# Strassen's products on twelve instead of eight of 32 channel blocks in both layers' ways out

## The chip, the cores and the metric

The kernel runs on one core of one Trainium2 chip. The metric is the device time of one execution in microseconds (us). The kernel before takes 1362.15 us, the median of 3 runs (1361.92 to 1362.23).

## What is computed

Two decoder layers on 256 tokens of width 2048, in float32:

```python
def retention_layer(x, g_norm, w_in, gn, w_out):
    ...                      # norm, q/k/v/gate projection, 8 heads of retention
    return o @ w_out         # (256 x 4096) @ (4096 x 2048)

def pooling_layer(x, g_norm, w_in, w_grp, b_grp, scale, w_out):
    ...                      # norm, branch/gate projection, causal pooling, 4 groups
    return (mix * jax.nn.silu(z)) @ w_out    # (256 x 4096) @ (4096 x 2048)

def reference(x, ...):
    h = x + retention_layer(x, ...)
    h = h + pooling_layer(h, ...)
    return rms_norm(h, final_norm)
```

The change concerns the two products with `w_out`, the "ways out" of the layers.

## The kernel before, in words

Every float32 value that a matmul reads is split in a rounded high part (a CAST on ScalarE, L98) and the rest (a subtract on VectorE, L99), and a product of two such pairs takes three matmuls: high by high, high by low, low by high (`Sum.add`, L195). Weights come in units of 128 x 2048 values, one DMA of 1 MB each, and a plain unit is split in two halves of 1024 columns. The pairs live in five rotating buffers (`w`), the raw units in three.

A way out (`way_out`) has two passes, one for each half of the 2048 output columns, and each pass sixteen units in the order of the string `ORDER`:

- A **C unit** holds four blocks of 128 channels by 512 columns. It goes to one column quarter: four blocks, two halves of the tokens (t), three matmuls each, so 24 matmuls of 512 columns.
- An **S unit** holds two blocks of channels by two column quarters, as the four corners of a two by two product with the two token halves (t). Strassen's way in Winograd's form takes seven products instead of eight: 21 matmuls in place of 24. VectorE pays for it: sums of weights (`s`, L221, 1024 columns; L223 and L224, 512 columns each), and four pairs (1024, 512, 1024 and 1024 columns) in place of two (1024 each).
- The sums of the activations that S units need (`forms`) are made once for each layer, in the first pass, by `sides` (L198 to L215), one call for two S units: an add of 1024 columns (L202), then four adds or subtracts of 256 columns (L208 to L214) and four splits of 256 columns (L99 again).

The eight sums of a pass (`p1`, `p5`, `p6`, `p7`, `c11`, `c21`, `c12`, `c22`) take all eight PSUM banks. After the last S unit VectorE adds the p's and two of the c's into the residual stream `xn` (`add`, L481, and L517, L520), while TensorE works on the C units that are left; these go to `c12` and `c22`, whose adds come last. In layer 1 each piece of 512 columns that is complete is squared and then turned by TensorE for the next layer (`turn`, L554 and L562). In layer 2 the last two C units are held and multiplied token half by token half, and each piece goes through the final norm (`norm`, L664 to L692, with a multiply on GpSimd, L671).

Before layer 1's way out stands the last head of the retention, whose output `og` TensorE turns (L453) for the blocks 28 to 31 of `os`. The buffer `tmp`, which `sides` writes first (L202), lies in memory that was `gz` and its neighbours in the heads, so that `sides` starts after those last turns. Instructions of one engine run in the order in which a scheduler has put them when the program was built; a read or write that depends on another engine waits on a semaphore.

Of the kernel before, what the change touches and what calls it, by code (L numbers as in the profile page):

```python
# [13 lines left out]
P = 128  # L14
# [11 lines left out]
UNIT = 2048  # L26
HALF = UNIT // 2

ORDER = "CCCCSCSCCSCSCCCC"
NS = ORDER.count("S")  # L30
CLASSIC = ((0, 0), (0, 1), (1, 0), (2, 0), (3, 0), (1, 1), (4, 0), (5, 0), (2, 1), (3, 1), (4, 1), (5, 1))
FIRST = (20, 16)
SUMS = ("p1", "p5", "p6", "p7", "c11", "c21", "c12", "c22")


# [15 lines left out]
def kernel(  # L51
# [44 lines left out]
    def split(hi, lo, src):  # L96

        nc.scalar.copy(hi, src)  # L98
        nc.vector.tensor_tensor(out=lo, in0=src, in1=hi.bitcast(F32), op=ALU.subtract)  # L99
# [87 lines left out]
    class Sum:  # L187
# [5 lines left out]
        def add(self, a_hi, a_lo, w_hi, w_lo):  # L193
            for a, w in ((a_hi, w_hi), (a_hi, w_lo), (a_lo, w_hi)):
                nc.tensor.matmul(self.tile, a, w, start=(self.done == 0), stop=(self.done == self.n - 1))  # L195
                self.done += 1

    def sides(A, first, i, a, s, forms):  # L198


        blocks = A[:, first + 4 * i : first + 4 * i + 4]
        nc.vector.tensor_tensor(out=a, in0=blocks[:, :, 0].bitcast(F32), in1=blocks[:, :, 1].bitcast(F32), op=ALU.add)  # L202
        a11, a21, a12, a22 = a[:, :2, :P], a[:, :2, P:], a[:, 2:, :P], a[:, 2:, P:]

        def put(form, src):
            split(forms[:, 2 * i : 2 * i + 2, form, 0], forms[:, 2 * i : 2 * i + 2, form, 1], src)

        nc.vector.tensor_tensor(out=s, in0=a21, in1=a22, op=ALU.subtract)  # L208
        put(0, s)
        nc.vector.tensor_tensor(out=a21, in0=a11, in1=a21, op=ALU.subtract)  # L210
        put(2, a21)
        nc.vector.tensor_tensor(out=s, in0=s, in1=a11, op=ALU.subtract)
        put(1, s)
        nc.vector.tensor_tensor(out=s, in0=s, in1=a12, op=ALU.add)  # L214
        put(3, s)  # L215
# [37 lines left out]
    with tc.tile_pool(name="rt", bufs=1) as rt:  # L253
# [62 lines left out]
        unit = 4  # L316


        forms = os[:, VT - 4 :].rearrange("p k a s -> p (k a s)").rearrange("p (i f l t) -> p i f l t", f=4, l=2, t=P)

        def tokens(k, t):
            ts = slice(t * P, (t + 1) * P)
# [137 lines left out]
    def way_out(A, src, first, forms, tmp, work, y, after, ends=False):  # L460
# [4 lines left out]
        def blk(k, t):  # L465
            ts = slice(t * P, (t + 1) * P)
            return A[:, k, 0, ts], A[:, k, 1, ts]

        for p in range(2):
# [20 lines left out]
            for n, kind in enumerate(ORDER):  # L490
                unit = src[p * len(ORDER) + n]
                if kind == "C":
                    u = (next(classic), weights(unit))
                    if ends and p == 1 and n >= len(ORDER) - 2:
                        held.append(u)
                    else:
                        rows(u, 0)
                        rows(u, 1)
                    if p == 0 and n in (1, 3):
                        a = tmp[:, : 4 * S].rearrange("p (k s) -> p k s", s=S)  # L500
                        sides(A, first, n // 2, a, tmp[:, 4 * S : 4 * S + 2 * P].rearrange("p (k s) -> p k s", s=P), forms)
                    if not ends and n == 5:
                        for c in (2 * p, 2 * p + 1):
                            tc.keep_in_program_order(nc.gpsimd.dma_start(out=y(None, c), in_=xN[:, :, c * 512 : (c + 1) * 512]))
                    continue
                raw = load(unit)
                s = [work.tile([P, 2, 512], F32, tag=f"s{i}", name=f"s{i}") for i in range(2)]
                k1, k2 = strassen_blocks(first, strassen)
                strassen_unit(raw, s, (blk(k1, 0), blk(k2, 0), blk(k2, 1)), forms[:, strassen], sums)
                strassen += 1  # L510
                if strassen == NS:
                    u = tmp[:, 4 * S + 2 * P :]
                    nc.scalar.copy(u, sums["p1"].tile)
                    add(0, 0, ALU.add, sums["c11"].tile)
                    add(0, 0, ALU.add, u)
                    after(0, 2 * p)
                    nc.vector.tensor_tensor(out=u, in0=u, in1=sums["p6"].tile, op=ALU.add)  # L517
                    add(0, 1, ALU.subtract, u)
                    add(1, 0, ALU.add, sums["c21"].tile)
                    nc.vector.tensor_tensor(out=u, in0=u, in1=sums["p7"].tile, op=ALU.add)  # L520
                    add(1, 0, ALU.add, u)
                    after(1, 2 * p)
                    add(0, 1, ALU.add, sums["p5"].tile)
                    add(1, 1, ALU.add, sums["p5"].tile)
                    add(1, 1, ALU.subtract, u)
# [10 lines left out]
    with tc.tile_pool(name="pl", bufs=1) as pl:  # L536
# [8 lines left out]

        with tc.tile_pool(name="work1", bufs=1) as work:
            tmp = pl.tile([P, 4 * S + 2 * P + 512], F32, tag="gz", name="tmp")
            forms = pl.tile([P, NS, 4, 2, P], F32R, tag="ms", name="forms")
            hs2 = act.tile([P, KT, 2, S], F32R, tag="hs", name="hs2")

            def turn(t, c):
                y = stream(t, c)
# [139 lines left out]
                nc.sync.dma_start(out=out[t][:, ps], in_=piece)  # L692

        with tc.tile_pool(name="work2", bufs=1) as work:
            tmp = act.tile([P, 4 * S + 2 * P + 512], F32, tag="hs", name="tmp")
            forms = pl.tile([P, NS, 4, 2, P], F32R, tag="ms", name="forms")
            way_out(gs, pool_out, FIRST[1], forms, tmp, work, stream, norm, True)


# [119 lines left out]
```

## Time and profile before

| what | value |
|---|---|
| median of 3 runs | 1362.15 us |
| the profiled execution's own time | 1361.73 us |
| its span, first to last instruction | 1359.4 us |
| PE busy | 1347.6 us, 99% |
| DVE (VectorE) busy | 1073.6 us, 79% |
| ACT (ScalarE) busy | 731.6 us, 54% |
| POOL (GpSimd) busy | 25.5 us, 2% |

The profile's engines are PE (TensorE), DVE (VectorE), ACT (ScalarE), POOL (GpSimd) and SP (the queue that issues loads). Successive instructions overlap a little, so a group's busy time is longer than its share of the engine; where an engine runs without a pause, the time from one start to the next start is what an instruction costs. The clock that was granted to TensorE is given for each stretch as a share of its full 2.4 GHz.

### The profile page before, as it was taken

The page shows a single profiled execution, that of the slowest core. Times are in us where ns is not written, and L with a number is a line of the kernel's source. Part 1 is how long each engine was busy: PE and PEld are TensorE (multiplying, and loading weights), DVE is VectorE, ACT ScalarE, POOL GpSimd, SP SyncE. Part 2 cuts the span into 40 slices and gives each one's busy share as a digit, 9 for nine tenths or more (in the row PEclk, how much of TensorE's full clock was granted, in tenths as well). Part 3 has the DMA queues.
Part 4 walks back from the last instruction along what each step waited for, and adds up shares of the span by engine and source line. Part 5 has one row for each costly group of instructions (what it writes and reads, how often), then busy time and mean ns, then how long its engine had stood idle before and what let it go on. Part 6 is the DMA issues. An engine that isn't in the chain of part 4 may idle for free.

```text
span 1359.4 us, 17755 instructions
## 1 busy us (share of the span) xinstructions
PE 1347.6 (99%) x6846; PEld 1145.6 (84%) x6846; DVE 1073.6 (79%) x1550; ACT 731.6 (54%) x1031; POOL 25.5 (2%) x34
## 2 busy tenths in 40 slices
PE   9999999999999999999999999999999999999997
PEld 7888888888888888878888888888888888888886
DVE  7868787878787878798677867876886896888676
ACT  7455555555555555555555545445545545555444
POOL 0000000000000000000000000000000000000102
PEclk9999999999999999999999999999999999999999
DMA  8555546464645455575556555555555555555552
GB/s 338 182 192 174 203 164 213 161 217 161 213 164 200 171 193 177 188 247 201 181 185 213 188 190 187 190 200 190 196 190 186 187 188 192 191 207 212 186 214 95
DMA packets 38196, 262.64 MB, mean 193 GB/s; under 512 B 4368, under 2 KB 4496, under 8 KB 7392
## 3 DMA queue, kind: packets, MB, share of 16 engines
q1 hardware_dynamic: 36432, 255.41, 54.3%
q0 software_dynamic: 1536, 5.57, 1.3%
q8 instruction: 54, 0.88, 0.2%
q10 hardware_dynamic: 144, 0.52, 0.1%
q14 instruction: 30, 0.25, 0.0%
HBM read 259.39 MB, written 2.10 MB: 192 GB/s over the span
## 4 chain that ended last, share of the span: by engine, by line
PE 98%; DVE 1%; ACT 0%; DMA 0%; issue 0%; DVEq 0%; SPq 0%; ACTq 0%
PE c L195 43%; PE acc L129 29%; PE acc L130 15%; PE p L195 6%; PE po L427 1%; PE acc L286 1%; PE acc L287 1%; PE turned L453 1%; PE sc L352 0%; DMA xin<-in_ret_in 0%; PE sc L357 0%; ACT w L98 0%; PE turned L562 0%; DVE w L99 0%; DVE tsin L339 0%; DVE tcos L338 0%
## 5 line engine op out<-in xcount | busy, mean ns | idle before, releaser
L99 DVE TENSOR_TENSOR w<-raw,w 128x1024 fp32r<-128x1024 f32 x472 | 558.1, 1192 | 140.7 <-ACT w L98 136.4
L98 ACT CAST w<-raw 128x1024 fp32r<-128x1024 f32 x472 | 479.1, 1026 | 275.5 <-PE c L195 172.8
L129 PE MATMUL acc<-hs,w 128*128 128x512 f32 x1472 | 516.3, 394 | 0.0
L130 PE MATMUL acc<-hs,w 128*128 128x256 f32 x1472 | 413.4, 281 | 0.0
L129 PEld LDWEIGHTS acc<-hs,w 128*128 128x128 f32 x1472 | 275.7, 187 | 61.8
L195 PE MATMUL c<-w,hs 128*128 128x512 f32 x1284 | 303.9, 390 | 0.0
L195 PEld LDWEIGHTS c<-w,hs 128*128 128x128 f32 x1284 | 239.1, 188 | 49.6
L130 PEld LDWEIGHTS acc<-hs,w 128*128 128x128 f32 x1472 | 278.0, 189 | 1.8
L195 PE MATMUL c<-w,os 128*128 128x512 f32 x666 | 162.6, 392 | 0.0
L195 PE MATMUL c<-w,gs 128*128 128x512 f32 x624 | 147.1, 390 | 0.0
L195 PEld LDWEIGHTS c<-w,os 128*128 128x128 f32 x666 | 124.4, 188 | 26.8 <-ACT w L98 0.3
L195 PEld LDWEIGHTS c<-w,gs 128*128 128x128 f32 x624 | 117.0, 188 | 24.8
L138 ACT COPY hl<-acc 128x256 f32<-128x256 f32 x96 | 35.6, 372 | 147.2 <-PE acc L130 147.2
L129 PE MATMUL acc<-ms,w 128*128 128x512 f32 x256 | 89.0, 390 | 0.0
L130 PE MATMUL acc<-ms,w 128*128 128x256 f32 x256 | 72.2, 282 | 0.0
L98 ACT CAST w<-s 128x1024 fp32r<-128x1024 f32 x32 | 33.5, 1049 | 53.9 <-PE c L195 48.6
L99 DVE TENSOR_TENSOR w<-s,w 128x1024 fp32r<-128x1024 f32 x32 | 39.1, 1223 | 24.6 <-ACT w L98 24.5
L129 PEld LDWEIGHTS acc<-ms,w 128*128 128x128 f32 x256 | 48.0, 188 | 10.1
L130 PEld LDWEIGHTS acc<-ms,w 128*128 128x128 f32 x256 | 48.4, 189 | 0.0
L195 PE MATMUL p<-w,os 128*128 128x512 f32 x150 | 40.9, 390 | 0.0
L195 PE MATMUL p<-w,forms 128*128 128x512 f32 x144 | 39.8, 397 | 0.5 <-ACT forms L98 0.5
L195 PEld LDWEIGHTS p<-w,forms 128*128 128x128 f32 x144 | 27.0, 188 | 7.5 <-ACT forms L98 1.0
(184 smaller groups left out, 1024.7 us busy)
## 6 DMA issues: line engine op xcount, KB each, us to landing
raw<-in_ret_in SPq DMA_DIRECT2D x92, 1024.0 KB, 5.0
raw<-in_pool_in SPq DMA_DIRECT2D x64, 1024.0 KB, 5.0
raw<-in_ret_out SPq DMA_DIRECT2D x32, 1024.0 KB, 5.0
raw<-in_pool_out SPq DMA_DIRECT2D x32, 1024.0 KB, 5.1
raw<-in_pool_grp SPq DMA_DIRECT2D x16, 1024.0 KB, 5.0
xin<-in_ret_in SPq DMA_DIRECT2D x3, 1024.0 KB, 11.4
xn<-in_xN POOLq DMA_DIRECT2D x4, 512.0 KB, 6.8
out<-xn SPq DMA_DIRECT2D x8, 256.0 KB, 2.3
```

The source lines that it names most:

```text
L98: nc.scalar.copy(hi, src)
L99: nc.vector.tensor_tensor(out=lo, in0=src, in1=hi.bitcast(F32), op=ALU.subtract)
L129: nc.tensor.matmul(acc, hi, moving[:, k], start=(k == 0), stop=False)
L130: nc.tensor.matmul(acc[:, :S], lo, moving[:, k, 0], start=False, stop=(k == n - 1))
L138: nc.scalar.copy(t, acc[:, S:])
L195: nc.tensor.matmul(self.tile, a, w, start=(self.done == 0), stop=(self.done == self.n - 1))
L286: nc.tensor.matmul(accs[c], hi[:, b], hs[:, k], start=(k == 0), stop=False)
L287: nc.tensor.matmul(accs[c][:, :S], lo[:, b], hs[:, k, 0], start=False, stop=(k == KT - 1))
L427: nc.tensor.matmul(po[t], ss[:, p, queries], vs[:, keys, q], start=first, stop=last)
L453: nc.tensor.transpose(turned[:, j * S + t * P : j * S + (t + 1) * P], og[:, t, (2 * i + j) * P : (2 * i + j + 1) * P], idt)
```

## The change

The order of a pass goes from twelve C units and four S units to ten and six, with the two in turn in the middle. The first and the last units of a pass stay plain, three and two of them in place of four and four. The S units' channel blocks now begin at 16 (layer 1) and 12 (layer 2). A third call of `sides` makes the forms of the added pair; in layer 1 these lie in the part of `hs2` that layer 2's input fills later, in layer 2 forms and `tmp` have changed places. The calls of `sides` come after the units 0, 2 and 4 of the first pass, in place of 1 and 3, and the load of `x` after unit 4 in place of 5.

```diff
-ORDER = "CCCCSCSCCSCSCCCC"
+ORDER = "CCCSCSCSCSCSCSCC"
 NS = ORDER.count("S")
-CLASSIC = ((0, 0), (0, 1), (1, 0), (2, 0), (3, 0), (1, 1), (4, 0), (5, 0), (2, 1), (3, 1), (4, 1), (5, 1))
-FIRST = (20, 16)
+CLASSIC = ((0, 0), (0, 1), (1, 0), (2, 0), (3, 0), (1, 1), (2, 1), (4, 0), (3, 1), (4, 1))
+FIRST = (16, 12)
...
+    def forms_at(blocks):
+        return blocks.rearrange("p k a s -> p (k a s)").rearrange("p (i f l t) -> p i f l t", f=4, l=2, t=P)
...
-            split(forms[:, 2 * i : 2 * i + 2, form, 0], forms[:, 2 * i : 2 * i + 2, form, 1], src)
+            split(forms[:, :, form, 0], forms[:, :, form, 1], src)
...
-                    if p == 0 and n in (1, 3):
+                    if p == 0 and n in (0, 2, 4):
                         a = tmp[:, : 4 * S].rearrange("p (k s) -> p k s", s=S)
-                        sides(A, first, n // 2, a, ..., forms)
-                    if not ends and n == 5:
+                        sides(A, first, n // 2, a, ..., forms[n // 2])
+                    if not ends and n == 4:
...
-            forms = pl.tile([P, NS, 4, 2, P], F32R, tag="ms", name="forms")
+            forms = pl.tile([P, 4, 4, 2, P], F32R, tag="ms", name="forms")
             hs2 = act.tile([P, KT, 2, S], F32R, tag="hs", name="hs2")
+            forms = [forms[:, :2], forms[:, 2:], forms_at(hs2[:, 8:12])]
...
-            tmp = act.tile([P, 4 * S + 2 * P + 512], F32, tag="hs", name="tmp")
-            forms = pl.tile([P, NS, 4, 2, P], F32R, tag="ms", name="forms")
+            tmp = pl.tile([P, 4 * S + 2 * P + 512], F32, tag="ms", name="tmp")
+            forms = act.tile([P, 6, 4, 2, P], F32R, tag="hs", name="forms")
+            forms = [forms[:, 2 * i : 2 * i + 2] for i in range(3)]
```

The added lines shift the numbers behind L198 by four or five: L202 is L206 in the changed kernel, L453 is L457, L481 is L485, L562 is L567.

**First place.** TensorE, layer 1's first pass, around the last turns of the retention (L453, in the changed kernel L457). `turned` is what TensorE writes when it turns `og`; `p1`, `p5` and `p7` are sums of the first S unit, `c11` and `c21` sums that C units share. Before:

```order
L453 MATMUL turned_4648<-idt_297,og_4641 128x128 x3
L453 MATMUL turned_4657<-idt_297,og_4641 128x128 x3
L195 MATMUL c21_4683<-w_4768,os_352 128x512 x3
L195 MATMUL c11_4682<-w_4797,os_352 128x512 x6
L195 MATMUL c11_4682<-w_4800,os_352 128x512 x6
L195 MATMUL c21_4683<-w_4797,os_352 128x512 x6
L195 MATMUL c21_4683<-w_4800,os_352 128x512 x6
L195 MATMUL p1_4678<-w_4845,os_352 128x512 x3
L195 MATMUL c11_4682<-w_4850,os_352 128x512 x3
L195 MATMUL p5_4679<-w_4853,forms_4676 128x512 x2
```

The change:

```order
L195 MATMUL c21_4683<-w_4768,os_352 128x512 x5
L457 MATMUL turned_4648<-idt_297,og_4641 128x128
L457 MATMUL turned_4657<-idt_297,og_4641 128x128
L195 MATMUL c21_4683<-w_4768,os_352 128x512
L457 MATMUL turned_4648<-idt_297,og_4641 128x128 x3
L457 MATMUL turned_4657<-idt_297,og_4641 128x128 x3
L195 MATMUL p1_4678<-w_4813,os_352 128x512 x3
L195 MATMUL c11_4682<-w_4818,os_352 128x512 x3
L195 MATMUL p5_4679<-w_4821,forms_4676 128x512 x2
L195 MATMUL p7_4681<-w_4821,forms_4676 128x512 x2
```

Between the last turn and the first matmul that reads `forms` stood 33 matmuls; now 6 stand there, and three of the others come ahead of the turns.

**Second place.** TensorE, the end of layer 1's second pass and the start of layer 2's first projection (`acc`, L129 and L130); `turned` (L562, now L567) is a piece of `xn`. Before, from the last C unit on:

```order
L195 MATMUL c22_5322<-w_5872,os_352 128x512 x6
L195 MATMUL c22_5322<-w_5875,os_352 128x512 x6
L129 MATMUL acc_5953<-hs2_4677,w_5947 128x512
L130 MATMUL acc_5953<-hs2_4677,w_5947 128x256
...
L562 MATMUL turned_5908<-idt_297,xn_4670 128x128
L562 MATMUL turned_5917<-idt_297,xn_4670 128x128
...
L562 MATMUL turned_5908<-idt_297,xn_4670 128x128 x3
L562 MATMUL turned_5917<-idt_297,xn_4670 128x128 x3
L129 MATMUL acc_5953<-hs2_4677,w_5950 128x512
```

The change:

```order
L195 MATMUL c22_5351<-w_5920,os_352 128x512 x6
L567 MATMUL turned_5871<-idt_297,xn_4670 128x128
L567 MATMUL turned_5862<-idt_297,xn_4670 128x128 x3
L567 MATMUL turned_5871<-idt_297,xn_4670 128x128 x3
L567 MATMUL turned_5953<-idt_297,xn_4670 128x128
L567 MATMUL turned_5962<-idt_297,xn_4670 128x128
L567 MATMUL turned_5953<-idt_297,xn_4670 128x128 x3
L567 MATMUL turned_5962<-idt_297,xn_4670 128x128 x3
L129 MATMUL acc_5998<-hs2_4677,w_5992 128x512
L130 MATMUL acc_5998<-hs2_4677,w_5992 128x256
```

The turns that stood between matmuls of the next projection now stand ahead of its first one, so that the projection waits for the adds into `xn` that the turns read.

**Third place.** VectorE, the same end of layer 1: the subtracts of weights (L99) and the adds of the evacuation, up to the add of `c22`. Before:

```order
L481 TENSOR_TENSOR xn_4670<-xn_4670,p5_5316 128x512 x2
L481 TENSOR_TENSOR xn_4670<-xn_4670,tmp_4675 128x512 x2
L99 TENSOR_TENSOR w_5875<-raw_5870,w_5875 128x1024
L99 TENSOR_TENSOR w_5947<-raw_5945,w_5947 128x1024
L99 TENSOR_TENSOR w_5950<-raw_5945,w_5950 128x1024
L104 SCALAR_TENSOR_TENSOR hs2_4677<-turned_5753,vec_70,hs2_4677 128x256
L104 SCALAR_TENSOR_TENSOR hs2_4677<-turned_5762,vec_70,hs2_4677 128x256
L99 TENSOR_TENSOR w_6025<-raw_6023,w_6025 128x1024
...
L481 TENSOR_TENSOR xn_4670<-xn_4670,c12_5321 128x512
L481 TENSOR_TENSOR xn_4670<-xn_4670,c22_5322 128x512
```

The change:

```order
L485 TENSOR_TENSOR xn_4670<-xn_4670,p5_5345 128x512 x2
L485 TENSOR_TENSOR xn_4670<-xn_4670,tmp_4675 128x512
L485 TENSOR_TENSOR xn_4670<-xn_4670,c12_5350 128x512
L485 TENSOR_TENSOR xn_4670<-xn_4670,tmp_4675 128x512
L99 TENSOR_TENSOR w_6073<-raw_6068,w_6073 128x1024
L99 TENSOR_TENSOR w_6121<-raw_6119,w_6121 128x1024
L485 TENSOR_TENSOR xn_4670<-xn_4670,c22_5351 128x512
L104 SCALAR_TENSOR_TENSOR hs2_4677<-turned_5862,vec_70,hs2_4677 128x256
```

The add of `c12` now stands inside the adds of the p's, and that of `c22` two subtracts behind them.

## Rows read from the trace of the kernel before

**Rows 1.** The page: busy us and share of the span, then the chain that ended last.
```profile
PE 1347.6 (99%) x6846; PEld 1145.6 (84%) x6846; DVE 1073.6 (79%) x1550; ACT 731.6 (54%) x1031; POOL 25.5 (2%) x34
...
PE 98%; DVE 1%; ACT 0%; DMA 0%; issue 0%; DVEq 0%; SPq 0%; ACTq 0%
```

**Rows 2.** Windows: stretch, us, busy us (count) of PE, PEld, DVE, ACT, POOL, then clock.
```profile
577.00:585.00 8.00, 8.00 (x36) 6.57 (x35) 8.00 (x13) 4.31 (x8) 2.86 (x4) 1.00 0.72 198
585.00:600.00 15.00, 14.48 (x62) 11.13 (x61) 14.63 (x21) 10.01 (x14) 0.00 (x0) 1.00 0.67 246
600.00:622.00 22.00, 22.00 (x98) 18.05 (x97) 18.75 (x25) 10.58 (x14) 0.00 (x0) 1.00 0.69 238
622.00:640.00 18.00, 18.00 (x81) 14.79 (x80) 17.06 (x20) 10.33 (x14) 0.00 (x0) 1.00 0.63 215
660.00:700.00 40.00, 40.00 (x177) 32.84 (x176) 28.06 (x28) 19.86 (x21) 0.00 (x0) 1.00 0.52 184
```

**Rows 3.** DVE's timeline, layer 1, first pass: start, us, engine, line, operation [idle before].
```profile
576.83 1.23 DVE L202 TENSOR_TENSOR tmp<-os 128x1024 f32<-128x1024 f32 x1 [0.27 <-PE turned L453]
...
582.70 0.68 DVE L224 TENSOR_TENSOR s<-s,raw 128x512 f32<-128x512 f32 x1
583.30 0.48 DVE L104 SCALAR_TENSOR_TENSOR os<-turned,vec,os 128x256 fp32r<-128x256 f32 x1
...
585.16 0.42 DVE L99 TENSOR_TENSOR forms<-tmp,forms 128x256 fp32r<-128x256 f32 x1
585.50 0.42 DVE L212 TENSOR_TENSOR tmp<-tmp 128x256 f32<-128x256 f32 x1
...
586.97 2.35 DVE L99 TENSOR_TENSOR w<-raw,w 128x1024 fp32r<-128x1024 f32 x2
589.24 0.42 DVE L99 TENSOR_TENSOR forms<-tmp,forms 128x256 fp32r<-128x256 f32 x1
```

**Rows 4.** PE's timeline of the same stretch.
```profile
576.50 6.41 PE L195 MATMUL c<-w,os 128*128 128x512 f32 x27
...
584.11 1.32 PE L195 MATMUL p<-w,forms 128*128 128x512 f32 x5
...
586.77 0.84 PE L195 MATMUL p<-w,forms 128*128 128x512 f32 x2 [0.52 <-ACT forms L98]
...
588.39 3.84 PE L195 MATMUL c<-w,os 128*128 128x512 f32 x16
```

**Rows 5.** Waits, 565 to 745 us: engine, line, what for, us, times, longest.
```profile
ACT w L98 <- PE c L195: 65.9, 44, 3.5
```

**Rows 6.** PE's timeline, end of layer 1's second pass.
```profile
711.52 5.61 PE L195 MATMUL c<-w,os 128*128 128x512 f32 x24
716.97 0.27 PE L562 MATMUL turned<-idt,xn 128*128 128x128 f32 x1
...
738.78 0.82 PE L562 MATMUL turned<-idt,xn 128*128 128x128 f32 x6
```

**Rows 7.** DVE's timeline of the same stretch.
```profile
708.89 1.23 DVE L99 TENSOR_TENSOR w<-raw,w 128x1024 fp32r<-128x1024 f32 x1 [1.55 <-ACT w L98]
...
734.90 0.69 DVE L481 TENSOR_TENSOR xn<-xn,c 128x512 f32<-128x512 f32 x1 [1.71 <-PE c L195]
```

**Rows 8.** Windows of layer 2's first pass, columns as in rows 2.
```profile
1222.00:1245.00 23.00, 23.00 (x102) 18.82 (x101) 16.95 (x19) 12.79 (x14) 0.00 (x0) 1.00 0.53 198
```

**Rows 9.** Timeline of the kernel's end, DVE and ACT.
```profile
1331.28 2.20 DVE L99 TENSOR_TENSOR w<-raw,w 128x1024 fp32r<-128x1024 f32 x1
...
1345.67 0.69 DVE L481 TENSOR_TENSOR xn<-xn,c 128x512 f32<-128x512 f32 x1 [3.08 <-PE c L195]
...
1348.36 1.95 ACT L688 ACTIVATE xn<-xn,rs_r 128x512 f32<-128x512 f32 x3 [0.85 <-DVE rs_r L172]
...
1351.83 0.63 ACT L664 ACTIVATE sqn<-xn 128x512 f32<-128x512 f32 x1 [1.52 <-DVE xn L481]
```

**Rows 10.** Window after the last matmul, columns as in rows 2.
```profile
1352.00:1359.00 7.00, 0.00 (x0) 0.00 (x0) 2.22 (x8) 1.57 (x4) 1.26 (x1) 0.75 0.50 189
```

More of the change, by code (lines that the diff above doesn't have):

```diff
@@ L316 @@
         unit = 4
-        forms = os[:, VT - 4 :].rearrange("p k a s -> p (k a s)").rearrange("p (i f l t) -> p i f l t", f=4, l=2, t=P)
+        forms = forms_at(os[:, VT - 4 :])
         def tokens(k, t):
@@ L498, in way_out @@
                         rows(u, 1)
-                    if p == 0 and n in (1, 3):
+                    if p == 0 and n in (0, 2, 4):
                         a = tmp[:, : 4 * S].rearrange("p (k s) -> p k s", s=S)
-                        sides(A, first, n // 2, a, tmp[:, 4 * S : 4 * S + 2 * P].rearrange("p (k s) -> p k s", s=P), forms)
-                    if not ends and n == 5:
+                        sides(A, first, n // 2, a, tmp[:, 4 * S : 4 * S + 2 * P].rearrange("p (k s) -> p k s", s=P), forms[n // 2])
+                    if not ends and n == 4:
                         for c in (2 * p, 2 * p + 1):
@@ L508, in way_out @@
                 k1, k2 = strassen_blocks(first, strassen)
-                strassen_unit(raw, s, (blk(k1, 0), blk(k2, 0), blk(k2, 1)), forms[:, strassen], sums)
+                strassen_unit(raw, s, (blk(k1, 0), blk(k2, 0), blk(k2, 1)), forms[strassen // 2][:, strassen % 2], sums)
                 strassen += 1
```

## Prediction

> **What bounds the kernel now.** I read the page first. TensorE (PE) is busy 99% of the span and carries 98% of the chain that ended last; VectorE (DVE) is busy 79% [rows 1]. So a matmul less should be 0.227 us less: the 24 of a C unit take from 711.52 to 716.97, 5.45 us [rows 6]. But 79% is an average. I therefore cut layer 1's way out in windows. In the first pass DVE has 8.00 of 8.00 us to do from 577, 14.63 of 15 from 585, 18.75 of 22, then 17.06 of 18; only in the second pass is there room, 28.06 of 40 from 660. In the second window PE drops to 14.48 of 15, the only one of these in which it pauses [rows 2]. The timelines say why: `sides` and the first S unit's sums queue on DVE from 576.83 on [rows 3], PE lives from matmuls prepared earlier, then meets its first `forms` at 584.11, and waits for a form at 586.77 [rows 4]. There the two engines touch already.
>
> **What an instruction costs.** PE: 0.227 us a matmul, so C 5.45 and S (21) 4.77. DVE, from starts without a pause between them: 1024 columns 1.14 (two from 586.97 to 589.24), 512 columns 0.60 (582.70 to 583.30), 256 columns 0.34 (585.16 to 585.50) [rows 3]. A C unit has two wide subtracts, 2.28; an S unit four wide and three of 512, 4 x 1.14 + 3 x 0.60 = 6.36; a call of `sides` one wide and eight narrow, 1.14 + 8 x 0.34 = 3.86. A pair of S and C asks 10.22 of PE and 8.64 of DVE; with a `sides` in it 12.50 of DVE.
>
> **The sum, place by place.**
>
> *Matmuls.* The order holds 24 fewer, six in each of four passes: -1.36 a pass, -5.45 in all.
>
> *Layer 1, first pass, start: +4.8.* DVE's first `sides` add waits for the last turns of the retention (it started 0.27 us after them, at 576.83 [rows 3]), and from there DVE's order up to the first C subtract behind S is, as printed, the same in both kernels. What PE has meanwhile is not: 33 matmuls before the first `forms` (the 27 at 576.50 and six more [rows 4]), now 6, since the fourth leading C unit is gone and three matmuls moved ahead of the turns. These three make everything on DVE 3 x 0.227 = 0.68 later. PE would run out at about 577.2 + 6 x 0.227 = 578.6 and wait until 584.11 + 0.68 = 584.8, some 6 us. The next place at which PE depends on DVE is the low half of the C unit behind, at 588.39 before [rows 4], so 589.07 now. Counted in the orders, 256 matmuls of the pass were left there before, now 274: +18 x 0.227 + 0.68 = +4.8, the pass's own -1.36 in it. If DVE hid this after all, it would be -1.36.
>
> *The same pass, further on: +2.0.* PE leaves that place with no lead. Two calls of `sides` are still to come, one more than before, each in a pair where DVE has 12.50 to do against 10.22: a deficit of 2.28. Pairs without one give back 1.58. The lower bound is one deficit less one such gain, +0.7, the upper two deficits uncushioned, +4.6. I walked the two orders against each other with these prices and take 2.0.
>
> *Layer 1, second pass: -1.4.* In the stretch from 660, which has pairs in turn, DVE has 12 of 40 us free [rows 2], and the casts wait 65.9 us in all for PE to free a weight buffer [rows 5]: the alternation is paid from slack.
>
> *End of layer 1: +3.2.* After the last S unit came four C units, 21.8 us of PE; now two, 10.9 us. The evacuation keeps its length. Before, the first of these subtracts started at 708.89, 2.63 before S ended at 711.52 [rows 6, 7]; the `c22` add waited 1.71 for PE (start 734.90 [rows 7]), so DVE was not late, and the last six turns stood behind several matmuls of the next projection (738.78 [rows 6]). Now nine wide subtracts and eleven adds stand on DVE from the same point to the `c22` add: 9 x 1.14 + 11 x 0.60 = 16.9, so it starts 14.3 and ends 14.9 behind the S unit. PE is through at 10.9 plus 0.8 for the turns that can go ahead, and all other turns stand ahead of the first matmul of the projection: 14.9 - 11.7 = 3.2 of waiting. Bounds: 1.0, should two of the subtracts get done earlier, and 4.3, should one more wide operation slip in.
>
> *Layer 2: -2.7.* Two passes of -1.36. In its first pass DVE shows 16.95 of 23 [rows 8], the start has no late turns in front, and by the same walk DVE stays some 3 us ahead. The new wait (`tmp` now takes the memory of `ms`) is for the last matmuls of the projection before, which lie ahead of the pass anyway. Bounds: -2.7, and 0 if the third `sides` (3.86) eats that lead.
>
> *The end of the kernel: +1.5.* The same shortening: `c12` is complete 5.45 before PE ends, and its add came at 1345.67, after 3.08 of waiting for PE [rows 9]. Now four subtracts and ten adds of 512 from 1.5 before S ends make it start at about 8.5 to 9.0 behind S, where PE completes `c12` at 5.45. One of the subtracts may take 2.20 instead of 1.22, as at 1331.28 beside GpSimd's multiply [rows 9]. The first token half then leaves ScalarE (three scalings, 1.95 from 1348.36) about 3 us later, and the second half's square, which started at 1351.83 [rows 9] with 1.52 of idle time ahead of it, is pushed by 3 - 1.5 = 1.5. Bounds 0 and 3.
>
> Sum: 4.8 + 2.0 - 1.4 + 3.2 - 2.7 + 1.5 = +7.4. The profiled execution took 1361.73, which gives 1369.1; the median of the runs is 0.42 above it, so **1369.5**. All low bounds together (4.1 at the start) give +1.3 or so, all high ones +15.
>
> **The rivals.**
>
> *A. The cover suffices, faster.* What decides is whether PE waits at the first `forms` of layer 1. If DVE's work there could be done ahead of the turns, PE would never stop and the change would give -5.45: 1356.7. For it: 79% on DVE, and the long waits of the casts for PE [rows 5], which are spare time. Against: DVE is full from 576.83 [rows 2], its first `sides` add waits for the turns, and the S unit's own sums stand behind that add in DVE's order. Chance 0.08.
>
> *B. Only the lost cover.* The start costs its 4.8, the pass after it its lower 0.7, the matmuls give 4.1 in the other passes, and both evacuations fit: +1.4, 1363.6. For it: DVE's waits before both last adds show 1.71 and 3.08 of room [rows 7, 9]. Against: that room is less than the 10.9 us of PE work taken away. Chance 0.13.
>
> *C. Layer 2 is DVE's as well.* The two pairs with `sides` in its first pass lose 2.3 each, less what the lead holds: +3 to +4 on the forecast, 1373. For it: the third `sides`; against: rows 8 show a quarter of DVE free. Chance 0.10.
>
> *D. TensorE's clock falls in the new wait.* The granted clock is 1.00 in every window of both passes [rows 2, 8], where PE never stops for as much as 1 us, and its mean is 0.75 in the 7.00 us after the last matmul [rows 10]: without work it did fall to the lower level. A wait of 6 us in layer 1 is the longest that this kernel would have between matmuls. At the lower level a matmul would take 0.454; the twelve until 589.07 then take 5.45 instead of 2.72, where DVE allows 4.3, +1.2, and a C unit behind them at that level adds up to 5.45 less what DVE's own pace hides, so some +3: 1372.5. Chance 0.10. The Trainium skill, "TensorE: Matmul & The Clock Gate", Part 1 (The HAM clock gate), says the same of idle time: the fast clock is granted only to a busy array, and after an idle stretch it is back at 1.2 GHz until it has been busy again. By that rule the stall costs more than its length, and D rather than the sum is the forecast; the trace of before has no stall long enough in mid-kernel to show it, so I leave it a rival.
>
> **How the numbers follow.** The forecast of 1369.5, with its terms in their ranges, has 0.59. A measurement of this kernel can tell about 0.2%, 2.7 us, from no change. A is faster: 0.08, with 0.01 of B. Within 2.7 us fall nearly all of B and a little of the forecast's low end: 0.13. Slower: 0.78. The range must hold 8 in 10: from B's 1363.5 up to C's and D's upper parts, 1374; A and the sum of all high bounds stay outside.
>
> **What would show it.** In the changed profile: a gap of about 6 us on PE ahead of the first `forms` matmul near 585, with DVE full beside it; small gaps until about 640; none in the second pass; one of about 3 us ahead of the first matmul of layer 2's projection, ended by an add into `xn` and its turns; matmuls 24 fewer. The second way out should be about 2.7 us shorter from its first matmul to its last. I am wrong if PE shows no gap near 580, if the gap is there and the clock beside it falls to the lower level, or if the second layer has gaps too.

## The result and the profile after

The changed kernel takes 1369.62 us (median of 4 runs, 1369.23 to 1370.48), the kernel before 1362.04 (4 runs, 1361.44 to 1362.23): slower by 0.57%, ratio 1.0057 with a 95% interval of 1.0043 to 1.0071. Its profiled execution took 1369.62 us with a span of 1367.8. The forecast was 1369.5, slower. The sum was met, but not each of its terms: one was far too small, two were too large, and one gain was in no term.

The page of the changed kernel, the rows that answer to [rows 1]:

```profile
PE 1347.7 (99%) x6822; PEld 1145.5 (84%) x6822; DVE 1115.4 (82%) x1608; ACT 746.0 (55%) x1055; POOL 28.3 (2%) x34
...
PE 94%; DVE 3%; ACT 1%; DMA 1%; issue 1%; DVEq 0%; SPq 0%; ACTq 0%
```

PE is 99% busy as before, so the share says nothing; what it carries of the chain fell from 98% to 94%, and DVE went from 79% to 82%. The windows of the stretches in [rows 2] and [rows 8] (busy us and count of PE, PEld, DVE, ACT, POOL, then the granted clock, DMA share, GB/s):

```profile
577.00:585.00 8.00, 3.18 (x16) 2.00 (x14) 7.09 (x12) 3.83 (x8) 2.85 (x4) 0.93 0.58 171
585.00:600.00 15.00, 15.00 (x53) 11.67 (x54) 14.43 (x21) 8.89 (x13) 0.00 (x0) 0.81 0.74 260
600.00:622.00 22.00, 20.89 (x90) 16.25 (x90) 21.76 (x28) 12.68 (x17) 0.00 (x0) 1.00 0.56 188
622.00:640.00 18.00, 18.00 (x81) 14.86 (x80) 17.68 (x23) 9.82 (x14) 0.00 (x0) 1.00 0.54 183
660.00:700.00 40.00, 40.00 (x180) 32.85 (x179) 33.62 (x40) 23.91 (x32) 0.00 (x0) 1.00 0.50 171
1222.00:1245.00 23.00, 23.00 (x103) 19.04 (x102) 22.68 (x30) 14.59 (x20) 0.00 (x0) 1.00 0.52 183
```

From 577 PE has 3.18 of 8 us to do where it had 8.00; from 585 it is busy without a break, but at a granted clock of 0.81, so with 53 matmuls where there were 62; from 600 it lacks 1.1 us more. From 660 and in layer 2's first pass it is full, with DVE now 33.62 of 40 and 22.68 of 23. The place of the wait that was forecast, on PE [rows 4] and on DVE [rows 3]:

```profile
578.35 0.86 PE L195 MATMUL c<-w,os 128*128 128x512 f32 x3
582.61 1.08 PE L195 MATMUL p<-w,forms 128*128 128x512 f32 x2 [3.40 <-issue]
585.00 1.62 PE L195 MATMUL p<-w,forms 128*128 128x512 f32 x3 [1.32 <-DVE os L104]
...
590.52 1.86 PE L195 MATMUL c<-w,os 128*128 128x512 f32 x7
```

```profile
577.91 1.23 DVE L206 TENSOR_TENSOR tmp<-os 128x1024 f32<-128x1024 f32 x1 [5.07 <-PE turned L457]
...
585.10 1.22 DVE L225 TENSOR_TENSOR s<-raw 128x1024 f32<-128x1024 f32 x1
```

The last of the six matmuls starts at 578.81 and the next one at 582.61 (3.8 us from start to start; the row counts 3.40 of idle time). PE gets out two matmuls and goes on at 585.00, some 6 us after it ran out. The trace puts the first wait down to "issue"; DVE beside it has not paused since 577.91. The first matmul that reads the next C unit's low half comes at 590.52; before, at 588.39.

The end of layer 1, DVE first (answers to [rows 7]), then PE ([rows 6]):

```profile
726.36 1.23 DVE L99 TENSOR_TENSOR w<-raw,w 128x1024 fp32r<-128x1024 f32 x1 [1.49 <-ACT w L98]
...
743.29 0.68 DVE L485 TENSOR_TENSOR xn<-xn,c 128x512 f32<-128x512 f32 x1
```

```profile
728.92 5.61 PE L195 MATMUL c<-w,os 128*128 128x512 f32 x24
...
740.40 1.14 PE L567 MATMUL turned<-idt,xn 128*128 128x128 f32 x9
744.03 1.34 PE L567 MATMUL turned<-idt,xn 128*128 128x128 f32 x6 [2.48 <-DVE xn L485]
745.92 0.77 PE L129 MATMUL acc<-hs,w 128*128 128x512 f32 x1 [0.55 <-DVE r L157]
```

The S unit ends at 728.92, the `c22` add starts 14.37 later; PE waits for it until 744.03 (2.8 us from start to start, 2.48 idle in the row) and once more until 745.92, before the first matmul of layer 2's projection. The six turns take 1.34 us where they took 0.82. The clock beside both waits:

```profile
583.00:585.00 2.00, 0.57 (x3) 0.22 (x2) 2.00 (x6) 0.91 (x2) 0.00 (x0) 0.71 0.98 283
585.00:590.00 5.00, 5.00 (x11) 3.56 (x12) 5.00 (x7) 3.79 (x5) 0.00 (x0) 0.50 0.96 352
590.00:593.00 3.00, 3.00 (x13) 2.39 (x12) 3.00 (x6) 0.00 (x0) 0.00 (x0) 0.89 0.51 142
745.00:747.00 2.00, 1.45 (x5) 1.01 (x4) 1.95 (x8) 1.72 (x5) 0.00 (x0) 0.50 0.72 299
747.00:750.00 3.00, 3.00 (x11) 2.52 (x11) 2.46 (x13) 0.76 (x2) 0.00 (x0) 0.50 0.00 0
750.00:752.00 2.00, 2.00 (x10) 1.72 (x10) 0.42 (x1) 0.77 (x2) 0.00 (x0) 0.72 0.00 0
752.00:754.00 2.00, 2.00 (x14) 1.74 (x13) 1.23 (x1) 0.41 (x1) 0.00 (x0) 1.00 0.00 0
```

It falls to the lower level (0.50, that is 1.2 GHz) at both places: between 583 and 585 and again by 745, behind the waits of 3.8 and 2.8 us, and is back about 590.7 and 751. In the kernel before the clock stays at 1.00 all through both ways out.

The end of the kernel, ScalarE and DVE (answers to [rows 9]):

```profile
1355.14 0.68 DVE L485 TENSOR_TENSOR xn<-xn,c 128x512 f32<-128x512 f32 x1
...
1357.98 1.95 ACT L693 ACTIVATE xn<-xn,rs_r 128x512 f32<-128x512 f32 x3 [0.85 <-DVE rs_r L172]
...
1359.84 0.61 ACT L669 ACTIVATE sqn<-xn 128x512 f32<-128x512 f32 x1
```

PE's last matmul starts at 1350.69 before and 1358.12 now. Seen from there the `c12` add is 2.0 us later than it was, the second half's square 0.6, the end of the span 0.9.

Where the 8.4 us of span come from, by the start of the same matmul in both traces: 0.4 are there at the first matmul that reads `os`, before any change; 5.3 more at the last matmul of layer 1's way out; another 7.3 at the 21st pair of the projection behind it (13.0 in all); between there and the end of its first group 1.7 are given back (11.3 left); in layer 2's way out 3.8; and 0.9 are lost behind the last matmul. Seven turns, 0.8 us, stood ahead of the second of these marks before and stand behind it now, so 0.8 of the 7.3 belong to the 5.3.

### The profile page after: what moved, and what is told of

The parts are those of the page before. It is cut to its first block, busy times and chain, and to the rows that moved or that the text cites. A ratio compares the mean times of both kernels' runs of the same rounds, so it can differ in the third digit from the quotient of the medians.

```text
span 1367.8 us, 17800 instructions
## 1 busy us (share of the span) xinstructions
PE 1347.7 (99%) x6822; PEld 1145.5 (84%) x6822; DVE 1115.4 (82%) x1608; ACT 746.0 (55%) x1055; POOL 28.3 (2%) x34
## 4 chain that ended last, share of the span: by engine, by line
PE 94%; DVE 3%; ACT 1%; DMA 1%; issue 1%; DVEq 0%; SPq 0%; ACTq 0%
PE c L195 39%; PE acc L129 29%; PE acc L130 15%; PE p L195 7%; PE po L431 1%; DVE w L99 1%; PE acc L290 1%; DVE xn L485 1%; PE acc L291 1%; PE turned L457 1%; PE sc L356 0%; DMA xin<-in_ret_in 0%; DMA raw<-in_ret_out 0%; ACT w L98 0%; PE sc L361 0%
## 5 line engine op out<-in xcount | busy, mean ns | idle before, releaser
L99 DVE TENSOR_TENSOR w<-raw,w 128x1024 fp32r<-128x1024 f32 x472 | 554.6, 1186 | 116.3 <-ACT w L98 112.0
L98 ACT CAST w<-raw 128x1024 fp32r<-128x1024 f32 x472 | 473.9, 1018 | 256.8 <-PE c L195 154.4
L129 PE MATMUL acc<-hs,w 128*128 128x512 f32 x1472 | 517.2, 394 | 0.6 <-DVE r L157 0.6
L130 PE MATMUL acc<-hs,w 128*128 128x256 f32 x1472 | 413.7, 281 | 0.0
L129 PEld LDWEIGHTS acc<-hs,w 128*128 128x128 f32 x1472 | 276.9, 188 | 62.6 <-PE turned L567 0.9
L130 PEld LDWEIGHTS acc<-hs,w 128*128 128x128 f32 x1472 | 278.9, 189 | 1.6
L195 PE MATMUL c<-w,os 128*128 128x512 f32 x594 | 149.5, 393 | 0.2 <-DVE w L99 0.2
L195 PE MATMUL c<-w,gs 128*128 128x512 f32 x552 | 133.6, 389 | 0.0
L195 PEld LDWEIGHTS c<-w,os 128*128 128x128 f32 x594 | 112.0, 189 | 24.9 <-DVE w L99 0.6
L195 PEld LDWEIGHTS c<-w,gs 128*128 128x128 f32 x552 | 103.5, 188 | 21.5
L129 PE MATMUL acc<-ms,w 128*128 128x512 f32 x256 | 89.0, 390 | 0.0
L98 ACT CAST w<-s 128x1024 fp32r<-128x1024 f32 x48 | 50.2, 1049 | 64.6 <-PE c L195 42.3
L130 PE MATMUL acc<-ms,w 128*128 128x256 f32 x256 | 72.2, 282 | 0.0
L99 DVE TENSOR_TENSOR w<-s,w 128x1024 fp32r<-128x1024 f32 x48 | 58.4, 1220 | 16.6 <-ACT w L98 16.6
L195 PE MATMUL p<-w,forms 128*128 128x512 f32 x180 | 51.8, 402 | 5.7 <-issue 3.4
L129 PEld LDWEIGHTS acc<-ms,w 128*128 128x128 f32 x256 | 48.0, 188 | 10.1
L130 PEld LDWEIGHTS acc<-ms,w 128*128 128x128 f32 x256 | 48.4, 189 | 0.0
L195 PEld LDWEIGHTS p<-w,forms 128*128 128x128 f32 x180 | 34.3, 192 | 15.0 <-issue 5.4
L195 PE MATMUL p<-w,os 128*128 128x512 f32 x162 | 45.3, 392 | 0.0
```

Source lines behind the costliest of these rows:

```text
L129: nc.tensor.matmul(acc, hi, moving[:, k], start=(k == 0), stop=False)
L130: nc.tensor.matmul(acc[:, :S], lo, moving[:, k, 0], start=False, stop=(k == n - 1))
```

## The experiments

Twelve kernels ran, with 5 to 11 executions each. In most of them `ORDER`, `CLASSIC`, `NS`, the places of `sides` and of the load of `x` are tables by layer and pass; the diffs show the main entries that differ from the changed kernel's. "Before" is the kernel before in the same comparison.

| run | median, us | before | ratio, 95% interval |
|---|---|---|---|
| l1_only | 1374.07 | 1362.52 | 1.0080 (1.0066 to 1.0093) |
| l2_only | 1358.70 | 1362.52 | 0.9971 (0.9960 to 0.9983) |
| warm | 1368.81 | 1362.52 | 1.0044 (1.0032 to 1.0057) |
| warm_start | 1368.92 | 1362.52 | 1.0042 (1.0029 to 1.0054) |
| lead | 1362.09 | 1362.21 | 0.9999 (0.9990 to 1.0007) |
| tail4 | 1365.17 | 1362.21 | 1.0022 (1.0012 to 1.0031) |
| aligned_before | 1362.98 | 1362.21 | 1.0007 (0.9998 to 1.0016) |
| best | 1361.13 | 1362.21 | 0.9990 (0.9981 to 0.9999) |
| forms_low | 1360.96 | 1362.13 | 0.9992 (0.9983 to 1.0001) |
| lead_tail | 1360.62 | 1362.13 | 0.9989 (0.9980 to 0.9998) |
| best2 | 1356.76 | 1362.13 | 0.9961 (0.9948 to 0.9973) |
| best3 | 1355.88 | 1361.92 | 0.9956 (0.9942 to 0.9969) |

**One layer at a time.** The new order in layer 1 alone:

```diff
-layer 2: ORDER "CCCSCSCSCSCSCSCC", FIRST 12, three calls of sides
+layer 2: ORDER "CCCCSCSCCSCSCCCC", FIRST 16, two calls of sides
```

> The new order in layer 1 alone, layer 2 as before. Theory (the losses are VectorE's, all in layer 1 and at the very end): layer 2's gain of 3.85 us between its first matmuls and its last and the 1.0 us lost behind the last matmul both go, so the time is 7.6 + 2.9 = some +10.5 us against the kernel before, about 1372.5. Rival (each further S unit costs more than it saves, wherever it stands): half of the change makes half of the loss, +3.8 us, 1365.8.

And in layer 2 alone:

```diff
-layer 1: ORDER "CCCSCSCSCSCSCSCC", FIRST 16, three calls of sides
+layer 1: ORDER "CCCCSCSCCSCSCCCC", FIRST 20, two calls of sides
```

> The new order in layer 2 alone, layer 1 as before. Theory: no pause on TensorE in layer 2, 2.7 us of matmuls saved, another 1.1 us from matmuls that run at 227 instead of 228 to 230 ns because forms lies elsewhere, 1.0 us lost behind the last matmul: -2.8 us against before, about 1359.2. Rival (each further S unit costs more than it saves): +3.8 us, 1365.8. If the faster matmuls of the changed kernel's layer 2 come from the clock's fall and return in layer 1 rather than from forms, they stay at 228 to 230 ns here and the time is 1360.3.

Measured +11.6 and -3.8 us: the change is a gain in one layer and a loss three times as large in the other, and the rival of a price for each S unit is out. In the trace of `l2_only` PE pauses nowhere in layer 2. At the end of the projection's first group it stands at +0.06 us against the kernel before, at the last matmul of all at -3.78; the changed kernel has 11.28 and 7.44 there. Both gain 3.84, so layer 1 changes nothing in layer 2's way out. Both effects were expected 1 us smaller. For `l1_only` the trace shows part of it: 1.6 us more than in the changed kernel are lost ahead of the first matmul that reads `os`, where this execution, the slowest of the five, had the clock at 0.50 from 9 to 12 us.

**The cover in front.** The fourth leading C unit is put back in layer 1's first pass:

```diff
-layer 1, first pass: "CCCSCSCSCSCSCSCC", sides after units 0, 2, 4
+layer 1, first pass: "CCCCSCSCSCSCSCSC", sides after units 0, 2, 5
```

> The changed kernel, but layer 1's first pass in the order CCCCSCSCSCSCSCSC: the fourth leading C unit is back (33 matmuls between the last turns and the first forms), and one C unit less closes the pass. Theory A (only the cover in front is missing): the loss of that place, 6.1 us plus the 1.0 us that the clock took, comes back, 1362.5. Theory B (VectorE's whole work up to the second S unit is the bound, it is busy without a break from the turns to 612 us, where TensorE waits last): only the two subtracts of the C unit that get done ahead of the turns, 2.3 us, and the 0.7 us of the turns come back, 1366.6, and TensorE waits later, between 590 and 612, instead.

```profile
576.87 6.41 PE L196 MATMUL c<-w,os 128*128 128x512 f32 x27
...
584.49 1.32 PE L196 MATMUL p<-w,forms 128*128 128x512 f32 x5
...
587.15 0.83 PE L196 MATMUL p<-w,forms 128*128 128x512 f32 x2 [0.51 <-ACT forms L99]
...
608.79 0.50 PE L196 MATMUL c<-w,os 128*128 128x512 f32 x1 [0.21 <-ACT w L99]
...
610.68 0.50 PE L196 MATMUL p<-w,os 128*128 128x512 f32 x1 [0.21 <-ACT w L99]
```

Theory A, against what I had come to expect: 7.5 us come back, as much as the whole change had cost. PE's timeline has its 27 matmuls again, meets `forms` at 584.49 and waits 0.51 there, as before [rows 4]. The waits that are left (608.79 and 610.68, two of nine small ones between 600 and 614) make some 2 us: that is the alternation's term. Against the changed kernel the projection starts 6.7 us earlier; the rest of the gain stands behind the wait at the end of layer 1, where the clock was low for some 3 us in this trace and some 7 in the changed kernel's. Theory B took DVE's unbroken work up to 612 for a bound of PE. In `lead` DVE is as busy (14.68 of 15 us from 585, 12.00 of 12 from 600), and PE waits some 2 us, not 7: full windows on DVE alone do not show that PE waits for it.

**The cover behind.** Four C units at the end of layer 1's second pass:

```diff
-layer 1, second pass: "CCCSCSCSCSCSCSCC"
+layer 1, second pass: "CSCSCSCSCSCSCCCC", its C units of the first quarter first
```

> The changed kernel, but layer 1's second pass in the order CSCSCSCSCSCSCCCC, so that four C units stand behind the last S unit as in the kernel before. Theory: the add of c22 waits for TensorE again, the turns stand between matmuls of the projection, no wait and no slow clock there: first matmul of the projection 11.2 - 5.7 = 5.5 us earlier, 2 us of half clock saved, less 0.6 us for turns behind it, 1369.6 - 6.9 = 1362.7. Rival (with a single C unit in front the second pass waits for VectorE at its start): 2 to 4 us of that are lost at the start of the second pass, 1365 to 1367.

```profile
742.25 0.69 DVE L489 TENSOR_TENSOR xn<-xn,c 128x512 f32<-128x512 f32 x1 [1.71 <-PE c L196]
```

The `c22` add waits 1.71 us for PE again, the very figure of [rows 7], and the turns stand between matmuls of the projection. The time falls by 4.5 against the changed kernel, not 6.9: 0.9 us is lost ahead of 633.67, where PE waits for the weights of the second pass's first S unit (the rival, in part), and the 1.7 us that the changed kernel wins back in the projection are not won here.

**Both covers.** The two edits together:

```diff
+layer 1, first pass: "CCCCSCSCSCSCSCSC"
+layer 1, second pass: "CSCSCSCSCSCSCCCC"
```

> The changed kernel with both covers back in layer 1: its first pass CCCCSCSCSCSCSCSC, its second CSCSCSCSCSCSCCCC; twelve blocks in both layers. Theory (the two losses are separate): 1369.6 - 7.5 for the lead - 4.4 for the tail = 1357.7, below the kernel with the change in layer 2 alone only if the 2.7 us of layer 1's matmuls outweigh what VectorE still delays. Rival (work taken off one place comes up at the other, here at the border of the passes, where two C units are left between two S units): a wait of 2 to 3 us near 635 us, 1360 to 1361.

```profile
656.60 0.87 PE L571 MATMUL turned<-idt,xn 128*128 128x128 f32 x6 [0.93 <-DVE xn L489]
...
660.07 1.18 PE L196 MATMUL c<-w,os 128*128 128x512 f32 x4 [0.44 <-DVE w L100]
```

The rival's time, 1360.6: with two C units between the passes the first pass's evacuation is late, and PE waits 0.93 before six turns and again behind them; by the starts of its matmuls some 3 us go there. I had expected that at 635; it is at 654 to 660. With ten C units a pass, cover that is put at one end was missed at the other.

**The clock.** Matmuls that nobody reads keep PE busy in the second wait:

```diff
+                if c == 3:
+                    warm = bank(4, "warm")
+                    for _ in range(14):
+                        nc.tensor.matmul(warm, ones, os[:, 0], start=True, stop=True)
```

> The changed kernel with 14 matmuls of 512 columns added whose result nobody reads, put by the scheduler before and between the last turns of layer 1, 9 of them at the wait for the last add. Theory (the clock's fall is a cost of its own at this place): TensorE is not idle for long there, the granted clock stays 1.00 behind it, the six turns and the first matmuls of the projection do not run at half speed: 0.7 + 2.2 = 2.9 us less than the changed kernel, 1366.7. Rival (the wait alone costs, and the slow matmuls hide other waits on VectorE): no change, 1369.6. If the added matmuls delay the turns, up to +1 us.

```profile
744.00:746.00 2.00, 0.48 (x5) 0.24 (x3) 2.00 (x8) 2.00 (x7) 0.00 (x0) 1.00 0.89 377
746.00:748.00 2.00, 1.73 (x10) 1.55 (x11) 1.90 (x9) 0.49 (x2) 0.00 (x0) 1.00 0.08 25
748.00:750.00 2.00, 2.00 (x13) 1.79 (x12) 1.15 (x7) 0.68 (x1) 0.00 (x0) 1.00 0.00 0
```

```profile
746.27 0.47 PE L130 MATMUL acc<-hs,w 128*128 128x512 f32 x1 [1.79 <-DVE hs L105]
```

The clock stays at 1.00, where the changed kernel shows 0.50. The ratio falls from 1.0057 to 1.0044, 1.8 us, with intervals that overlap, so the time alone does not show a gain. In the trace the lead over the changed kernel at the 21st pair is 2.3, 2.1 without a difference that is there from the start. That the clock's fall is a cost of its own agrees with this; its price, some 2 us in place of 2.9, rests on one pair of traces. PE still waits, 1.79 us for the high and low parts of the turned pieces, which the slow turns and matmuls had partly covered.

In the first wait:

```diff
+        for _ in range(17):   # layer 1, first pass, first S unit
+            nc.tensor.matmul(sums["p5"].tile, ones, hs[:, 0], start=True, stop=True)
         sums["p1"].add(*a11, *cut((b_hi, b_lo), 0))
```

> The changed kernel with 17 matmuls of 512 columns added whose result nobody reads, between the last turns of the retention and the first S unit, so that the wait of 3.8 us there is filled. Theory (TensorE follows VectorE here, but the fall of the clock still cost: the first dependence on the C unit behind came at 590.5 instead of the 589.5 that VectorE's order gives): granted clock 1.00 behind 585, 0 to 1.0 us less, 1369.1. Rival (the half clock is what the stretch from 585 to 600 loses, since its twelve matmuls and the next C unit run at 427 ns): 3 us less, 1366.6.

```profile
577.00:583.00 6.00, 6.00 (x31) 4.86 (x29) 5.21 (x8) 2.92 (x6) 2.85 (x4) 1.00 0.45 140
585.00:590.00 5.00, 4.09 (x15) 2.61 (x16) 5.00 (x7) 3.57 (x5) 0.00 (x0) 1.00 0.94 346
```

1.00 again, and with the wait at the end of layer 1 as it was the projection starts 0.8 us earlier: it is DVE more than the clock that sets the pace in the first wait, as expected. By the spans the run is 2.0 us shorter, because in this trace the clock after the second wait came back some 3 us earlier (by 748). The filler need not be the cause: in `lead`, which has none, the low stretch there is as short. The medians differ by less, 1.2 us against the kernel before in each comparison, and the intervals overlap.

**Where `forms` lies.** In layer 2's way out of the changed kernel matmuls run at 226.7 ns from start to start, in the kernel before at 228.2 on the mean, those on `forms` at 233. First guess: the kernel before begins `forms` 32 bytes behind a multiple of 64.

```diff
-        part2 = pl.tile([P, 2, 4], F32, name="part2")
+        part2 = pl.tile([P, 2, 8], F32, name="part2")[:, :, :4]
```

> The kernel before with 32 bytes more behind part2, so that forms and ms begin at a multiple of 64 bytes in each partition instead of 32 behind one; nothing else changes. Theory (matmuls that load their stationary operand from such a place take 233 ns instead of 227, and slow their neighbours): 1.1 us less in each layer's way out, 1360.0. Rival (the faster matmuls in the changed kernel's layer 2 have another cause, such as the order of the units): no change, 1362.2.

No gain, rather 0.8 us more, and `forms` still at 233. The trace shows where the 0.8 arises: the padding moves `ms` as well, and the 128 matmuls that read it in the first group take 22.49 us instead of 22.08, with 0.1 more in each later group. Second guess, the place itself:

```diff
-            tmp = act.tile([P, 4 * S + 2 * P + 512], F32, tag="hs", name="tmp")
-            forms = pl.tile([P, NS, 4, 2, P], F32R, tag="ms", name="forms")
+            tmp = pl.tile([P, 4 * S + 2 * P + 512], F32, tag="ms", name="tmp")
+            forms = act.tile([P, NS, 4, 2, P], F32R, tag="hs", name="forms")
```

> The kernel before, with four S units a pass, in whose layer 2 forms and tmp have changed places as in the changed kernel (forms in the memory of hs, 68 KB into the partition, tmp in that of ms, at 197 KB); nothing else changes. Theory (where forms lies sets how fast the matmuls that read it run; the multiple of 64 bytes has just been ruled out): matmuls on forms at 227 instead of 233 ns in layer 2, 1.0 us less, 1361.2. Rival (the order of the units makes them faster): 233 ns stay and the time is 1362.2.

The same seven matmuls of layer 2's last pass, in `aligned_before` and in `forms_low`:

```profile
1316.81 1.79 PE L195 MATMUL p<-w,forms 128*128 128x512 f32 x7
```

```profile
1315.60 1.75 PE L195 MATMUL p<-w,forms 128*128 128x512 f32 x7
```

1.79 against 1.75 for seven, that is 233 against 227 ns each (the last matmul's tail, 0.16, is in both figures), in a kernel whose code differs from the kernel before in the places alone. Its time is 1.2 us lower than that of the kernel before, and in the trace layer 2's way out is 0.9 shorter; the interval of the ratio just reaches 1. The scheduler's order differs too: the last 32 matmuls of the projection, which stood among the first C units, now stand ahead of them. `best3` below settles the place without this.

**Versions that beat both.** Six S units only where DVE has room:

```diff
+layer 1: "CCCCSCSCCSCSCCCC" (4 S, as before), then "CCSCSCSCSCSCSCCC" with the third sides behind its first unit
+layer 2: "CCCSCSCSCSCSCSCC", then "CCSCSCSCSCSCSCCC"
+part2 as in aligned_before
```

> S units only where VectorE has room: layer 1's first pass with four S units as before, its second pass with six in the order CCSCSCSCSCSCSCCC (the third call of sides moved to that pass's start), layer 2 with six and six, its second pass in the same order with three C units at the end; forms and ms at a multiple of 64 bytes. Theory: -3.8 us for layer 2 as measured alone, -1.4 for layer 1's second pass, -1.1 for the alignment in layer 1, up to -1 at the kernel's end, and 0 to +2 where three C units cover an evacuation less: 1355 to 1357. If the third sides or the shorter lead stalls TensorE, 1359.

1361.1, a miss. Three C units are too few at the end of layer 1: PE waits 1.3 us twice, the clock falls, and 3.5 us are lost between the last matmul of layer 1's way out and the first of the projection. The padding costs 1.7, twice what it cost above: the matmuls on `ms` take 22.49 us for 22.08 in all four groups. This execution was also the slowest of eleven, with the clock at 0.50 from 8 to 11 us, which cost some 1.5 us ahead of any change. So without the padding, and with four C units there:

```diff
-layer 1, second pass: "CCSCSCSCSCSCSCCC"; part2 padded
+layer 1, second pass: "CSCSCSCSCSCSCCCC"; part2 as before
```

> Layer 1: first pass with four S units in the order of the kernel before, second pass with six as CSCSCSCSCSCSCCCC, the third call of sides at that pass's start; layer 2: six and six, the second pass as CCSCSCSCSCSCSCCC. Theory: TensorE waits nowhere, 18 matmuls fewer, 1.1 us from forms in layer 2: -4.1 - 1.1 and some 0.4 lost behind the last matmul: 1357.4. Rival (the third sides at the start of the second pass, with one C unit in front of its first S unit, stalls TensorE there): 1359 to 1361.

1356.8, the theory's number within 0.7. PE pauses nowhere that the kernel before did not; the first matmul of the projection is 1.28 us earlier than before, the last matmul 5.0. Finally the forms of layer 1's first two pairs in the lower memory:

```diff
-            forms = [forms[:, :2], forms[:, 2:], forms_at(hs2[:, 8:12])]
+            forms = [forms_at(hs2[:, 8:12]), forms_at(hs2[:, 12:16]), forms[:, :2]]
```

> The last kernel (four and six S units in layer 1, six and six in layer 2), but the forms of layer 1's first two pairs lie in two parts of hs2, 100 and 84 KB into the partition or lower, and only the third pair's in the upper memory. Theory (the place of forms sets the pace of the matmuls that read it): 227 instead of 233 ns in layer 1 as well, another 0.5 to 0.8 us less, 1356.1. Rival (hs2 is free only later, or the scheduler's order turns out worse): 1356.8 or more.

```profile
686.37 1.75 PE L196 MATMUL p<-w,hs 128*128 128x512 f32 x7
...
696.63 1.80 PE L196 MATMUL p<-w,forms 128*128 128x512 f32 x7
```

1355.9, 0.44% under the kernel before and 1% under the changed one. In one pass of one kernel the S units whose forms lie in `hs` take 1.75 for seven matmuls and those in `forms` 1.80; in `best2`, where the pairs lie the other way round, so do the times:

```profile
687.50 1.80 PE L196 MATMUL p<-w,forms 128*128 128x512 f32 x7
...
697.78 1.75 PE L196 MATMUL p<-w,hs 128*128 128x512 f32 x7
```

## Why the prediction was right, step by step

- **Matmuls, 24 fewer, 0.227 each.** Right, -2.72 a layer; layer 1's part is inside the next two terms.
- **Start of layer 1's first pass, +4.8, and the alternation, +2.0, with -1.4 for the second pass.** Right: +5.4 forecast, +5.3 read at the last matmul of the way out, 6.0 with the turns that moved behind it. The mechanism is shown by `lead`: with 33 matmuls in front of `forms` the wait of 3.8 us is gone. The first `forms` were forecast for 584.8; two of their matmuls came from 582.61 on, since these read the form's high part only, which ScalarE had cast by 582.51; the rest came from 585.00 on. What was sized wrong there is small: C's low half at 590.5 and not 589.07. Of this 0.4 is from the start of the run; the rest is mostly the clock's, since DVE had the low half ready by 589.26 and PE came to it later, at 427 ns a matmul.
- **End of layer 1, +3.2.** The mechanism was right to a tenth: the add was forecast 14.3 us behind the S unit and started 14.37 behind it. The term was too small all the same: it measured 7.3, or 6.5 without the turns that moved. The wait itself was 2.7 from the end of one turn to the start of the next; behind it came, all missing from the sum, 0.8 of a second wait, for DVE's work on the turned pieces, 0.5 in six turns and some 2.4 in the projection's first matmuls, both at half clock.
- **Rival D, the clock.** It was given 0.10, and it happened, though with another price and mostly at another place. The prediction named it as a sign of being wrong, a gap near 580 with the clock beside it at the lower level, and by that sign it was wrong here, though the time came out as forecast. In the 6 us wait for which it was worked out it cost about 1 us, since PE follows DVE there (`warm_start`), not 3; at the shorter wait, which I had not thought of for it, about 2 (`warm`). The Trainium skill's page "TensorE: Matmul & The Clock Gate", Part 1 (The HAM clock gate), says that an idle array goes back to 1.2 GHz until it has been busy again; the 0.50 in the windows behind both waits agrees with it. The step that failed was to weigh the clock only against the longest wait, and to make it a rival where the sum already held waits.
- **Layer 2, -2.7.** PE pauses nowhere, as forecast, but the layer gained 3.84. The other 1.1 was in no term: the exchange of `tmp` and `forms`, which the diff shows and I priced as a wait alone, makes the matmuls on `forms` faster. `forms_low` gets 0.9 (trace) to 1.2 (median) without any S unit more.
- **The end, +1.5.** Mechanism right, size 0.9: the `c12` add came 2.0 later, not 3.
- **Given back in layer 2's first group, -1.7, in no term.** In the changed kernel matmuls of 512 columns there run at 231 ns where they ran at 236; 0.2 of the 1.7 are two matmuls of the norm that stand ahead of the mark now. The faster pace is in every run in which all turns stand ahead of the projection (`lead`, `warm`, `best` and the others), and in none with turns between its matmuls (`tail4`, `best2`, `l2_only`). Why was not tried further and stays open.

So 4.1 us too little at the end of layer 1, and 0.4 that stood there before any change, met 1.1, 1.7 and 0.6 too much elsewhere. The slower time and its place follow from the mechanism; that 1369.5 was hit within 0.2 us is luck. One side figure does not add up: the low bounds together give +1.7, not +1.3; nothing hangs on it. Rivals A and C are out: the start does wait, and layer 2 does not. B fails on the wait at the end of layer 1, where it had the evacuation fit.

## What to carry to other kernels

An engine that is 79% busy can still set the pace where its work comes in a lump behind a dependency: count what the other engine has left to do there, in its own order, and move work only into stretches in which the windows show room. A change of this kind is best made where it fits, a layer and a pass at a time: six S units in three of four passes, with the forms moved, take 5 to 6 us off; in all four they add 7.6. And each pause of PE should be checked for what it does to the clock behind it, above all where PE, not its supplier, sets the pace afterwards: here it cost about 1 us in the one case and about 2 in the other.

## What the runs showed of the hardware that was not expected

- The granted clock fell to half within the changed kernel behind waits of 3.8 and 2.8 us, and was back some 7 us later each time; matmuls of 512 columns then took 427 ns from start to start. In `lead` and `warm_start` it was back some 3 us after its fall at the end of layer 1. In `best` it fell behind two waits of 1.3 us with six turns between them; in `warm`, with one wait of 1.79 idle us, it stayed at 1.00.
- Matmuls with their stationary operand in a tile at 197 KB of the partition took 233 ns, at 68 to 100 KB 227, in the same kernel (`best3`, `best2`; the places follow from the sizes of the tiles). A start at a multiple of 64 bytes did not change it (`aligned_before`). Which property of the place it is stays open.
- A shift of 32 bytes in the upper tiles cost about 0.8 us (`aligned_before`, its interval reaches 1), in the trace nearly all of it in the matmuls whose moving operand is `ms`, one of the tiles that moved. In `best` the same shift cost 1.7 us there, 22.49 instead of 22.08 us for 128 matmuls in each of the four groups. The cause was not tried.
